# A gated short-convolution layer in fp32 halves: adaLN's scales and features moved directly behind their totals, the opening passes' products reordered, the first low part moved ahead, and the load of conv_w held back

## The chip, the cores and the metric

The kernel runs on one NeuronCore of one Trainium2 chip. The metric is the device time of one execution in microseconds (us), as the median of several runs. Before the change it is 913.54 us, the median of three runs (913.52 to 914.13).

## What is computed

The layer has one batch row, 256 positions, 2048 channels (`D`) and a branch width of 4096 (`E`). Cut to what matters, in NumPy-like words:

```python
h = rmsnorm(x, norm_g)                                   # (256, 2048)
shift, scale, gate = split(silu(c) @ ada_w + ada_b, 3)   # ada_w: (2048, 3*2048)
h = h * (1 + scale) + shift
b_gate, c_gate, v, g = split(h @ w_in, 4)                # w_in: (2048, 4*4096)
u = causal_conv3(c_gate * v, conv_w)                     # per channel, 3 taps
y = b_gate * u * silu(g)
out = rmsnorm(x + gate * (y @ w_out), final_g)           # w_out: (4096, 2048)
```

All tensors are fp32. `w_in` alone is 128 MB, so the weights are streamed once from HBM.

## The kernel before, in words

**Products in three parts.** Every weight tile that lands from HBM (`raw`, 128 rows by 2048 columns) is split into a high part (`hi`, a copy in the fp32r format on ACT, `high()`, line 603) and a low part (`lo = raw - hi` on DVE, `low()`, line 610). The features h are kept in the same way as a high and a low half of the tile `hT`. One product of a 128x128 weight block with 256 positions is then three matmuls: high weights by high features, high weights by low features, and low weights by high features (`product()`, line 507, the matmul itself is line 511). Every matmul has a weight load of its own.

**Why there are passes.** The features of channel block k (128 channels; there are 16) can only be made when the shift and the scale of that block are known, and these need their columns of `ada_w`, another 32 MB that come in during the first third of the kernel. So the first half of `w_in`'s columns is worked off in passes over the channel blocks whose features are ready: first k = 0 and 1 for every column group, then k = 2 and 3, and so on. `plan()` (line 75) fixes these passes. A pass is cut into pieces, one per weight tile, numbered b = 0, 1, 2, ...; pieces 0 and 1 are half tiles. A full piece has 48 matmuls for 128x1024 weights, in two halves of 24 (j = 0 and 1), each half into a PSUM bank of its own. The passes that begin at k = 0 are called opening passes here: pieces 0 to 9. Piece 9 is the first that uses k = 2 and 3; piece 14 is the first that uses k = 4 and 5.

**The order inside a half.** In the opening passes (`opening_products()`, line 528) a half does 16 matmuls with the high weights and then 8 with the low weights. In all later ones (`chunk_products()`, line 517) the three matmuls of one weight block follow one another: high, high, low, eight times.

**How features become ready.** `ada_w`'s columns for two channel blocks arrive in eight tiles (`at`); for each, `sum_one()` does two multiply-adds on DVE into `gv` (lines 487 and 489). When the eighth is done, `turn_sums()` puts four transposes on PE (`tp_g`, line 496), `total_sums()` sums the transposed rows on ACT (line 503), `all_scales()` makes scale and shift on DVE (lines 647 to 649), and `all_features()` makes the features: ACT writes the high half of `hT` (line 361), DVE the low half (lines 362 and 363). There are seven such groups of two channel blocks after the first, which is made at the start by another path (lines 398 to 443).

**What sets the order.** Each engine runs its instructions in the order of the program. The loop over pieces (line 731) writes this order out: it is pinned by `in_order()` until all features are made (line 782), and from there on a scheduler chooses. For piece b the loop makes the high part of piece b + 2, some sums, then the scales, the low part of piece b + 2, then the features, and then PE's matmuls for piece b; the transposes and totals come in the middle of the matmuls, after the first half. A clock per engine, kept by `spend()` with fixed costs, decides how many sums go between (`sum_some()`). All loads are issued on the SP queue. After piece 44 the loop also loads the taps `conv_w` as 96 rows of 512 bytes (`rows2`, line 784), and transposes them on PE (line 273) into `cw` (line 275); nothing on the way holds that load, so that the scheduler issues it near the start of the kernel.

After the passes the second half of `w_in`'s columns follows with all 16 channel blocks at once (`mm_b`), and then the product with `w_out` (`mm_o`).

Of the kernel before, what the change touches and what calls it, by code (L numbers as in the profile page):

```python
# [13 lines left out]
P = 128  # L14
# [47 lines left out]
SUM_US = 1.5  # L62
# [91 lines left out]
def short_conv_layer(ctx: ExitStack, tc: tile.TileContext, x, c, norm_g, ada_w, ada_b, w_in, conv_w, w_out, final_g, out):  # L154
# [204 lines left out]
    def features(k, sc, sh):  # L359
        hf = xs[k // CT][:, k % CT, :]  # L360
        nc.scalar.activation(hh_[:, k], hf, AF.Identity, bias=sh, scale=sc)
        nc.vector.tensor_scalar(out=hf, in0=hf, scalar1=sc, scalar2=sh, op0=ALU.mult, op1=ALU.add)
        nc.vector.tensor_tensor(out=hl_[:, k], in0=hf, in1=hh_[:, k].bitcast(F32), op=ALU.subtract)  # L363
# [70 lines left out]
    hi0 = wpool.tile([P, SLOT], F32R, tag="hi", name="hi", bufs=3)  # L434
    lo0 = wpool.tile([P, SLOT], F32R, tag="lo", name="lo", bufs=3)
    w = CT * P
    for k in range(NK0):
        nc.vector.tensor_tensor(out=sh_sc[:, k], in0=sums0[k][:, :, 0], in1=b_both[:, :, k], op=ALU.add)
    for k in range(NK0):
        c = slice(k * w, (k + 1) * w)  # L440
        nc.scalar.copy(hi0[:, c], raw0[:, c])
        nc.vector.tensor_tensor(out=lo0[:, c], in0=raw0[:, c], in1=hi0[:, c].bitcast(F32), op=ALU.subtract)
        features(k, sh_sc[:, k, 1:2], sh_sc[:, k, 0:1])

    def taps(ct, u, cv):

# [52 lines left out]
    def ada_total(nk, tp):  # L499

        gs = const.tile([P, 4], F32, tag="gs", name="gs", bufs=2)
        for o in range(2 * nk):
            nc.scalar.activation(tp[:, o, :], tp[:, o, :], AF.Copy, accum_out=gs[:, o : o + 1])
        return gs[:, 0:nk], gs[:, nk : 2 * nk]
# [130 lines left out]
    def total_sums():  # L635

        while totals:
            k0, nk, tp = totals.pop(0)
            whole_sums.append((k0, nk, ada_total(nk, tp)))
            spend("act", TOTAL_US, clock["pe"])  # L640

    def all_scales():

        while whole_sums:
            k0, nk, (sums_shift, sums_scale) = whole_sums.pop(0)
            ks = slice(k0, k0 + nk)
            nc.vector.tensor_tensor(out=scale[:, ks], in0=sums_scale, in1=b_scale1[:, ks], op=ALU.add)
            nc.vector.tensor_tensor(out=scale[:, ks], in0=scale[:, ks], in1=gT[:, ks], op=ALU.mult)
            nc.vector.tensor_tensor(out=shift[:, ks], in0=sums_shift, in1=b_shift[:, ks], op=ALU.add)
            spend("dve", STALL_US)  # L650
            scaled.append((k0, nk))

    def all_features():
# [77 lines left out]
    for b, (n, chs, q, k0, k1, seeds, w, s0, sk, _) in enumerate(flat):  # L731
        us = sk * len(chs) * CT * 3 * PRODUCT_US
        begin, end = clock["pe"], clock["pe"] + us
        last = s0 + sk == k1
        for e in ("dve", "act"):
            clock[e] = max(clock[e], begin)
        early = b + 2 < N and raws.get((b + 2, "at"), begin) > begin - EARLY_US
        for closing in (early, not early):
            if closing:
                if ended_pass is not None:  # L740
                    close_bank(ended_pass, len(passes[ended_pass][1]) - 1)
                    ended_pass = None
            else:
                nxt = b + 2 < N and high(b + 2)
        if nxt:
            sum_some(nxt[2] + STALL_US, HI_US)
            all_scales()
            low(b + 2, *nxt)
        all_features()
        get_ready(s0 + sk)  # L750
        if last and n + 1 in passes:
            open_bank(n + 1, 0)
            if len(chs) == 1 and len(passes[n + 1][1]) == 2:
                open_bank(n + 1, 1)
        adds = last and len(chs) == 2 and k0 > 0 and not seeds[0]
        sum_some(end + AHEAD_US, STALL_US)
        mix_some(end + AHEAD_US)
        hi, lo = parted.pop(b)
        parted[b] = None
        for j in range(len(chs)):  # L760
            bank = banks[n, j]
            if b == 0:
                for k in range(NK0):
                    chunk_products(bank, hi, lo, k * w, k, k0, k1, late=True)
            elif k0 == 0:
                opening_products(bank, hi, lo, w, j * CT * P, s0, sk, k1)
            else:
                for i in range(sk):
                    chunk_products(bank, hi, lo, i * w + j * CT * P, s0 + i, k0, k1, seeds[j])
            if j == 0:  # L770
                clock["pe"] = begin + us / len(chs)
                turn_sums(clock["pe"] - TURN_US)
                if last and len(chs) == 2:
                    close_bank(n, 0)
                    if n + 1 in passes:
                        open_bank(n + 1, 1)
                total_sums()
        clock["pe"] = end
        if last:
            ended_pass = n  # L780
        if ready[0] == KT:
            pinned.close()
        if b == CONV_AT:
            nc.sync.dma_start(rows2[:, :], conv_w.rearrange("w (k p) -> (w k) p", p=P))
            turn(rows2, 0, 96, cw)
    close_bank(ended_pass, len(passes[ended_pass][1]) - 1)
    for us, do in mixing:
# [221 lines left out]
```

## Time and profile before

| | |
|---|---|
| median of the runs | 913.54 us |
| profiled execution, device time | 913.98 us |
| profiled execution, span of the trace | 912.2 us |
| PE (matmuls) busy | 898.8 us, 99% |
| PE weight loads busy | 860.4 us, 94% |
| DVE busy | 632.9 us, 69% |
| ACT busy | 452.9 us, 50% |
| loaded from HBM | 224.48 MB |

The span is what the trace covers; the device time of the same execution is 1.8 us longer. A time with a dot and two decimals, such as 71.42, is a moment in us from the start of the span. A timeline row gives its start, its length, engine, line, operation, output and inputs and the number of instructions merged into it; in square brackets stands how long the engine sat idle before it and what ended that. PE is busy almost without a break, so the time is to be found in two places: in the few short waits of PE, and in the pace at which matmuls follow one another, which the busy share does not show because successive matmuls overlap.

### The profile page before, as it was taken

The page shows a single profiled execution, that of the slowest core. Times are in us where ns is not written, and L with a number is a line of the kernel's source. Part 1 is how long each engine was busy: PE and PEld are TensorE (multiplying, and loading weights), DVE is VectorE, ACT ScalarE, POOL GpSimd, SP SyncE. Part 2 cuts the span into 40 slices and gives each one's busy share as a digit, 9 for nine tenths or more (in the row PEclk, how much of TensorE's full clock was granted, in tenths as well). Part 3 has the DMA queues.
Part 4 walks back from the last instruction along what each step waited for, and adds up shares of the span by engine and source line. Part 5 has one row for each costly group of instructions (what it writes and reads, how often), then busy time and mean ns, then how long its engine had stood idle before and what let it go on. Part 6 is the DMA issues. An engine that isn't in the chain of part 4 may idle for free.

```text
span 912.2 us, 16163 instructions
## 1 busy us (share of the span) xinstructions
PE 898.8 (99%) x7045; PEld 860.4 (94%) x7045; DVE 632.9 (69%) x603; ACT 452.9 (50%) x430; POOL 1.8 (0%) x8
## 2 busy tenths in 40 slices
PE   7999999999999999999999999999999999999996
PEld 5999999999999999999999999999999988888885
DVE  5788899999646878776666666666566644555882
ACT  6688776545545755643344443334433433433333
POOL 0000000000000000000000000000000000000000
PEclk9999999999999999999999999999999999999999
DMA  9999999999555555797677778777877496565542
GB/s 307 382 381 357 314 364 338 321 345 312 190 197 202 190 190 184 256 299 247 216 255 239 240 219 270 248 238 227 255 239 245 145 356 203 199 204 191 185 139 92
DMA packets 146855, 227.63 MB, mean 250 GB/s; under 512 B 5456, under 2 KB 103904, under 8 KB 146400
## 3 DMA queue, kind: packets, MB, share of 16 engines
q1 hardware_dynamic: 146688, 226.56, 74.4%
q8 instruction: 55, 0.90, 0.4%
q14 instruction: 16, 0.13, 0.0%
q0 software_dynamic: 64, 0.02, 0.0%
q10 hardware_dynamic: 32, 0.01, 0.0%
HBM read 224.48 MB, written 2.10 MB: 248 GB/s over the span
## 4 chain that ended last, share of the span: by engine, by line
PE 91%; DMA 5%; DVE 2%; ACT 1%; issue 0%; ACTq 0%; SPq 0%
PE mm_b L511 38%; PE mm_s L511 33%; PE mm_o L907 6%; PE mm_o L906 6%; PE mm_o L905 6%; DMA at<-in_ada_w_dram 3%; DMA raw_s<-in_sc_w_in_dram 1%; DVE gv L489 1%; DVE lo L610 1%; DMA x<-in_x_dram 1%; ACT hi L603 0%; PE tp_g L496 0%; PE ps_gate L843 0%; DVE acc L545 0%; ACT big L919 0%
## 5 line engine op out<-in xcount | busy, mean ns | idle before, releaser
L511 PE MATMUL mm_b<-hT,hi 128*128 128x256 f32 x2048 | 348.4, 276 | 0.0
L511 PE MATMUL mm_s<-hT,hi 128*128 128x256 f32 x2048 | 338.4, 277 | 1.1 <-DVE hT L363 1.0
L511 PEld LDWEIGHTS mm_b<-hT,hi 128*128 128x128 f32 x2048 | 308.7, 188 | 0.1
L511 PEld LDWEIGHTS mm_s<-hT,hi 128*128 128x128 f32 x2048 | 300.4, 188 | 2.0 <-DVE hT L363 1.7
L511 PE MATMUL mm_b<-hT,lo 128*128 128x256 f32 x1024 | 282.6, 276 | 0.0
L511 PE MATMUL mm_s<-hT,lo 128*128 128x256 f32 x1024 | 263.2, 277 | 0.3 <-DVE lo L610 0.2
L370 DVE TENSOR_TENSOR lo<-raw,hi 128x2048 fp32r<-128x2048 f32 x64 | 146.7, 2292 | 114.9 <-ACT hi L369 114.9
L369 ACT CAST hi<-raw 128x2048 fp32r<-128x2048 f32 x64 | 122.4, 1913 | 197.7 <-PE mm_b L511 142.5
L511 PEld LDWEIGHTS mm_b<-hT,lo 128*128 128x128 f32 x1024 | 192.2, 188 | 0.0
L511 PEld LDWEIGHTS mm_s<-hT,lo 128*128 128x128 f32 x1024 | 183.4, 188 | 0.7 <-DVE lo L610 0.4
L610 DVE TENSOR_TENSOR lo<-raw_s,hi 128x2048 fp32r<-128x2048 f32 (+1 forms) x64 | 145.5, 2273 | 54.0 <-ACT hi L603 52.8
L603 ACT CAST hi<-raw_s 128x2048 fp32r<-128x2048 f32 (+1 forms) x64 | 121.5, 1899 | 105.8 <-PE mm_s L511 85.4
L370 DVE TENSOR_TENSOR lo<-raw_o,hi 128x2048 fp32r<-128x2048 f32 x32 | 73.3, 2290 | 63.6 <-ACT hi L369 63.6
L369 ACT CAST hi<-raw_o 128x2048 fp32r<-128x2048 f32 x32 | 61.0, 1907 | 106.4 <-PE mm_o L907 84.5
L906 PE MATMUL mm_o<-lo,y 128*128 128x512 f32 x256 | 99.3, 389 | 0.0
L907 PE MATMUL mm_o<-hi,y 128*128 128x512 f32 x256 | 99.3, 389 | 0.0
L905 PE MATMUL mm_o<-hi,y 128*128 128x512 f32 x256 | 99.3, 389 | 0.0
L489 DVE SCALAR_TENSOR_TENSOR gv<-at,silu_c,gv 128x512 f32<-128x512 f32 x105 | 78.8, 750 | 2.7
L906 PEld LDWEIGHTS mm_o<-lo,y 128*128 128x128 f32 x256 | 48.1, 188 | 10.0
L905 PEld LDWEIGHTS mm_o<-hi,y 128*128 128x128 f32 x256 | 48.1, 188 | 10.0
L907 PEld LDWEIGHTS mm_o<-hi,y 128*128 128x128 f32 x256 | 48.1, 188 | 9.9
L543 ACT COPY acc<-mm_s 128x1024 f32<-128x1024 f32 x43 | 43.2, 1013 | 12.7 <-PE mm_s L511 12.7
(106 smaller groups left out, 377.4 us busy)
## 6 DMA issues: line engine op xcount, KB each, us to landing
raw<-in_sc_w_in_dram SPq DMA_DIRECT2D x64, 1024.0 KB, 6.7
raw_s<-in_sc_w_in_dram SPq DMA_DIRECT2D x63, 1024.0 KB, 6.7
raw_o<-in_sc_w_out_dram SPq DMA_DIRECT2D x32, 1024.0 KB, 5.2
at<-in_ada_w_dram SPq DMA_DIRECT2D x126, 256.0 KB, 7.2
at_g<-in_ada_w_dram SPq DMA_DIRECT2D x32, 512.0 KB, 7.6
x<-in_x_dram SPq DMA_DIRECT2D x4, 512.0 KB, 6.5
big<-in_x_dram SPq DMA_DIRECT2D x2, 1024.0 KB, 7.5
out_dram<-big SPq DMA_DIRECT2D x4, 512.0 KB, 2.9
```

The lines of the kernel that those rows point to most:

```text
L369: nc.scalar.copy(hi[:, :n], raw[:, :n])
L370: last_low[0] = nc.vector.tensor_tensor(out=lo[:, :n], in0=raw[:, :n], in1=hi[:, :n].bitcast(F32), op=ALU.subtract)
L489: nc.vector.scalar_tensor_tensor(out=gv, in0=at4[:, i], scalar=c_k, in1=gv, op0=ALU.mult, op1=ALU.add)
L511: mm = last_mm[0] = nc.tensor.matmul(dst, w, h[:, k], start=begins and left, stop=ends, skip_group_check=True)
L543: nc.scalar.copy(acc[ch, q], bank)
L603: nc.scalar.copy(hi[:, :n], raws[b][:, :n])
L610: nc.vector.tensor_tensor(out=lo[:, :n], in0=raws.pop(b)[:, :n], in1=hi[:, :n].bitcast(F32), op=ALU.subtract)
L905: nc.tensor.matmul(po, yh, hi[:, o], start=opens, stop=False, skip_group_check=True)
L906: nc.tensor.matmul(po, yh, lo[:, o], start=False, stop=False, skip_group_check=True)
L907: nc.tensor.matmul(po, yl, hi[:, o], start=False, stop=ct == NCT - 1, skip_group_check=True)
```

## The change

Five things are done.

1. `all_scales()` and `all_features()` are called directly behind `total_sums()`, in the middle of piece b's matmuls, and no longer in the next turn of the loop around the low part of piece b + 2. `all_scales()` now knows when its totals are ready and first does such sums as fit in before (`at`).
2. With that, the rest of the sums (`sum_some(end + AHEAD_US, ...)`) and of the mixing (`mix_some`) move behind these calls, and a smaller part (`sum_some(begin + us / len(chs), ...)`) stays ahead of the matmuls.
3. `opening_products()` is only used for b + j < 4, that is for piece 1, both halves of piece 2 and the first half of piece 3. All later halves of the opening passes use `chunk_products()`.
4. For the first two channel blocks at the start, DVE makes the low weights of block 0 before the second sum, and not behind it.
5. The load of `conv_w`'s rows is ordered behind the last weight load issued so far.

```diff
-    for k in range(NK0):
+
+    def first_sums(k):
         nc.vector.tensor_tensor(out=sh_sc[:, k], in0=sums0[k][:, :, 0], in1=b_both[:, :, k], op=ALU.add)
-    for k in range(NK0):
+
+    def first_parts(k):
         c = slice(k * w, (k + 1) * w)
         nc.scalar.copy(hi0[:, c], raw0[:, c])
         nc.vector.tensor_tensor(out=lo0[:, c], in0=raw0[:, c], in1=hi0[:, c].bitcast(F32), op=ALU.subtract)
-        features(k, sh_sc[:, k, 1:2], sh_sc[:, k, 0:1])
+
+    first_sums(0)
+    first_parts(0)
+    first_sums(1)
+    features(0, sh_sc[:, 0, 1:2], sh_sc[:, 0, 0:1])
+    first_parts(1)
+    features(1, sh_sc[:, 1, 1:2], sh_sc[:, 1, 0:1])
...
-            whole_sums.append((k0, nk, ada_total(nk, tp)))
-            spend("act", TOTAL_US, clock["pe"])
+            whole_sums.append((k0, nk, ada_total(nk, tp), spend("act", TOTAL_US, clock["pe"])))
...
-            k0, nk, (sums_shift, sums_scale) = whole_sums.pop(0)
+            k0, nk, (sums_shift, sums_scale), at = whole_sums.pop(0)
+            while waiting and max(clock["dve"], waiting[0][2]) + SUM_US <= at + STALL_US:
+                sum_one()
...
-            spend("dve", STALL_US)
+            spend("dve", STALL_US, at)
...
             sum_some(nxt[2] + STALL_US, HI_US)
-            all_scales()
             low(b + 2, *nxt)
-        all_features()
         get_ready(s0 + sk)
...
-        sum_some(end + AHEAD_US, STALL_US)
-        mix_some(end + AHEAD_US)
+        sum_some(begin + us / len(chs), STALL_US)
...
-            elif k0 == 0:
+            elif k0 == 0 and b + j < 4:
                 opening_products(bank, hi, lo, w, j * CT * P, s0, sk, k1)
...
                 total_sums()
+                all_scales()
+                all_features()
+                sum_some(end + AHEAD_US, STALL_US)
+                mix_some(end + AHEAD_US)
...
-            nc.sync.dma_start(rows2[:, :], conv_w.rearrange("w (k p) -> (w k) p", p=P))
+            load = nc.sync.dma_start(rows2[:, :], conv_w.rearrange("w (k p) -> (w k) p", p=P))
+            tc.add_manual_dep(load.ins, last_load[0].ins.name, after, reason="behind this piece's load")
             turn(rows2, 0, 96, cw)
```

The number of matmuls, weight loads, vector and scalar operations and loads is the same before and after. What moves is shown at three places. The numbers behind names tell tiles of one name apart.

First PE, in pieces 3 and 4 (`hi_335` and `lo_343` are the weights of piece 3, `hi_375` and `lo_382` those of piece 4; `mm_s` are the banks). Before:

```order
L511 MATMUL mm_s_386<-hT_164,hi_335 128x256 x16
L511 MATMUL mm_s_386<-hT_164,lo_343 128x256 x8
L511 MATMUL mm_s_413<-hT_164,hi_335 128x256 x16
L511 MATMUL mm_s_413<-hT_164,lo_343 128x256 x8
L511 MATMUL mm_s_456<-hT_164,hi_375 128x256 x16
L511 MATMUL mm_s_456<-hT_164,lo_382 128x256 x8
```

The same place now, with repeated rows left out; the second half of piece 3 and all of piece 4 follow the pattern high, high, low:

```order
L519 MATMUL mm_s_386<-hT_164,hi_335 128x256 x16
L519 MATMUL mm_s_386<-hT_164,lo_343 128x256 x8
L519 MATMUL mm_s_413<-hT_164,hi_335 128x256 x2
L519 MATMUL mm_s_413<-hT_164,lo_343 128x256
...
L519 MATMUL mm_s_456<-hT_164,hi_375 128x256 x2
L519 MATMUL mm_s_456<-hT_164,lo_382 128x256
```

From the second half of piece 3 to the end of piece 9, thirteen halves change their order; a low weight block is now needed by the third matmul of a half and not by the seventeenth.

Second DVE, where the features of k = 4 and 5 are made (`gv_1073` and `gv_1100` are the sums of the group after, `lo_1156` and `lo_1133` the low part of piece 15, `lo_1067` that of piece 14). Before:

```order
L610 TENSOR_TENSOR lo_1067<-raw_s_863,hi_1064 128x2048
L487 TENSOR_SCALAR gv_1073<-at_930,silu_c_132 128x512
L489 SCALAR_TENSOR_TENSOR gv_1073<-at_930,silu_c_132,gv_1073 128x512
L489 SCALAR_TENSOR_TENSOR gv_1073<-at_941,silu_c_132,gv_1073 128x512 x2
L489 SCALAR_TENSOR_TENSOR gv_1073<-at_999,silu_c_132,gv_1073 128x512 x2
L647 TENSOR_TENSOR scale_170<-gs_1116,vec_130 128x2
L648 TENSOR_TENSOR scale_170<-scale_170,vec_130 128x2
L649 TENSOR_TENSOR shift_169<-gs_1116,vec_130 128x2
L610 TENSOR_TENSOR lo_1156<-raw_s_935,hi_1145 128x2048
L362 TENSOR_SCALAR xs1_166<-xs1_166,scale_170,shift_169 128x256
L363 TENSOR_TENSOR hT_164<-xs1_166,hT_164 128x256
```

The same place now:

```order
L618 TENSOR_TENSOR lo_1062<-raw_s_858,hi_1059 128x2048
L497 SCALAR_TENSOR_TENSOR gv_712<-at_897,silu_c_132,gv_712 128x512 x2
L495 TENSOR_SCALAR gv_1100<-at_962,silu_c_132 128x512
L497 SCALAR_TENSOR_TENSOR gv_1100<-at_962,silu_c_132,gv_1100 128x512
L618 TENSOR_TENSOR lo_1133<-raw_s_930,hi_1130 128x2048
L656 TENSOR_TENSOR scale_170<-gs_1166,vec_130 128x2
L657 TENSOR_TENSOR scale_170<-scale_170,vec_130 128x2
L658 TENSOR_TENSOR shift_169<-gs_1166,vec_130 128x2
L362 TENSOR_SCALAR xs1_166<-xs1_166,scale_170,shift_169 128x256
L363 TENSOR_TENSOR hT_164<-xs1_166,hT_164 128x256
```

The low part of piece 15 has gone from between the scales and the features to ahead of the scales, and the last two sums of this group (`gv_712`) now stand behind the low part of piece 14. With that, PE's four transposes for this group move back by one piece: they stood in the middle of piece 12, and stand in the middle of piece 13 now, 24 matmuls ahead of the first that needs k = 4. Those of the first group (k = 2 and 3) stay in the middle of piece 7.

Third the SP queue, at the load of `conv_w`'s rows. Before, it stood near the start:

```order
L583 DMA raw_s_277<-in_sc_w_in_dram 128x2x512
L583 DMA raw_s_279<-in_sc_w_in_dram 128x2x1024
L474 DMA at_281<-in_ada_w_dram 128x2x256 x2
L583 DMA raw_s_284<-in_sc_w_in_dram 128x2x1024
L474 DMA at_286<-in_ada_w_dram 128x2x256 x2
L784 DMA rows2_83<-in_sc_conv_w_dram 96x128
L583 DMA raw_s_293<-in_sc_w_in_dram 128x2x1024
```

Now it stands directly behind the load of piece 49 (`raw_s_3163`):

```order
L591 DMA raw_s_2996<-in_sc_w_in_dram 128x2x1024
L591 DMA raw_s_3055<-in_sc_w_in_dram 128x2x1024
L591 DMA raw_s_3109<-in_sc_w_in_dram 128x2x1024
L591 DMA raw_s_3163<-in_sc_w_in_dram 128x2x1024
L794 DMA rows2_83<-in_sc_conv_w_dram 96x128
L591 DMA raw_s_3221<-in_sc_w_in_dram 128x2x1024
```

It has passed 46 weight loads and all later `at` loads on that queue. The transpose of these rows on PE, which stood between pieces 44 and 45, now stands behind the first matmul of piece 46.

## The prediction

> **What bounds the kernel now.** The page comes first: its span, and the busy shares.
>
> ```profile
> span 912.2 us, 16163 instructions
> PE 898.8 (99%) x7045; PEld 860.4 (94%) x7045; DVE 632.9 (69%) x603; ACT 452.9 (50%) x430; POOL 1.8 (0%) x8
> ```
>
> PE has no idle time to speak of, so what can be won is its few waits and its pace. The waits of PE between 30 and 381 us (the stage the change touches) are these three, 1.2 us in all:
>
> ```profile
> PE mm_s L511 <- DVE hT L363: 1.0, 2, 0.8
> PE mm_s L511 <- DVE lo L610: 0.2, 1, 0.2
> ```
>
> The pace shows in the busy time by stretches (length, then PE busy with its instructions):
>
> ```profile
> 40.00:50.00 10.00, 10.00 (x86) 10.00 (x86) 9.02 (x9) 7.58 (x7) 0.00 (x0) 1.00 1.05 381
> 272.00:381.00 109.00, 109.00 (x964) 109.00 (x963) 79.76 (x83) 65.72 (x64) 0.00 (x0) 1.00 0.62 203
> ```
>
> Both stretches are full at a granted clock of 1.00, yet the first runs 8.6 matmuls per us and the second 964 / 109 = 8.84. The timeline of PE shows where pace and waits change (start, length):
>
> ```profile
> 30.71 2.09 PE L511 MATMUL mm_s<-hT,hi 128*128 128x256 f32 x16
> ...
> 39.78 2.16 PE L511 MATMUL mm_s<-hT,hi 128*128 128x256 f32 x16
> ...
> 42.72 2.04 PE L511 MATMUL mm_s<-hT,hi 128*128 128x256 f32 x16
> ...
> 45.54 2.04 PE L511 MATMUL mm_s<-hT,hi 128*128 128x256 f32 x16
> ...
> 62.86 2.13 PE L511 MATMUL mm_s<-hT,hi 128*128 128x256 f32 x16
> ...
> 65.77 2.04 PE L511 MATMUL mm_s<-hT,hi 128*128 128x256 f32 x16
> ...
> 68.60 2.04 PE L511 MATMUL mm_s<-hT,hi 128*128 128x256 f32 x16
> ...
> 71.42 0.28 PE L511 MATMUL mm_s<-hT,hi 128*128 128x256 f32 x1
> 71.96 1.99 PE L511 MATMUL mm_s<-hT,hi 128*128 128x256 f32 x15 [0.26 <-DVE hT L363]
> ...
> 74.70 1.98 PE L511 MATMUL mm_s<-hT,hi 128*128 128x256 f32 x16
> ...
> 77.42 0.39 PE L511 MATMUL mm_s<-hT,hi 128*128 128x256 f32 x2
> ...
> 91.02 0.60 PE L496 MATMUL tp_g<-ident,gv 128*128 128x128 f32 x4
> 91.38 0.48 PE L511 MATMUL mm_s<-hT,hi 128*128 128x256 f32 x2
> ...
> 92.53 0.39 PE L511 MATMUL mm_s<-hT,hi 128*128 128x256 f32 x2
> ...
> 92.87 0.39 PE L511 MATMUL mm_s<-hT,hi 128*128 128x256 f32 x2
> ...
> 99.67 0.28 PE L511 MATMUL mm_s<-hT,hi 128*128 128x256 f32 x1
> 100.70 0.39 PE L511 MATMUL mm_s<-hT,hi 128*128 128x256 f32 x1 [0.75 <-DVE hT L363]
> ...
> 101.04 0.40 PE L511 MATMUL mm_s<-hT,hi 128*128 128x256 f32 x2
> ```
>
> A half of 24 matmuls takes 45.54 - 42.72 = 2.82 us in piece 4, and 77.42 - 74.70 = 2.72 us in piece 9, in the same old order. So there are two paces, 118 and 113 ns per matmul. The slow one holds until the wait at 71.42, and the fast one from there.
>
> **The features moved forward, pieces 9 and 14.** Piece 9's first half takes 74.70 - 71.42 = 3.28 us, 0.56 over 2.72. Piece 14 loses more: three matmuls from 99.67 to 101.04 take 1.37 where 3 x 0.113 = 0.34 is due, a loss of 1.03. On DVE the reason stands in the rows, a low part in front of the features:
>
> ```profile
> 68.83 2.29 DVE L610 TENSOR_TENSOR lo<-raw_s,hi 128x2048 fp32r<-128x2048 f32 x1 [0.44 <-ACT hi L603]
> 71.48 0.43 DVE L363 TENSOR_TENSOR hT<-xs,hT 128x256 fp32r<-128x256 f32 x1
> ...
> 97.24 0.15 DVE L647 TENSOR_TENSOR scale<-gs,vec 128x2 f32<-128x2 f32 x1
> ...
> 97.51 0.16 DVE L649 TENSOR_TENSOR shift<-gs,vec 128x2 f32<-128x2 f32 x1
> 97.58 2.29 DVE L610 TENSOR_TENSOR lo<-raw_s,hi 128x2048 fp32r<-128x2048 f32 x1
> 99.78 0.41 DVE L362 TENSOR_SCALAR xs<-xs,scale,shift 128x256 f32<-128x256 f32 x1
> 100.22 0.42 DVE L363 TENSOR_TENSOR hT<-xs,hT 128x256 fp32r<-128x256 f32 x1
> ```
>
> For piece 9 the change takes that low part (2.29 us) and the four sums ahead of it out of the way, while the transposes stay in the middle of piece 7, before 62.86. The features come some 4 us ahead of PE and the wait goes: **0.56 us gained**. Next late there would be piece 9's low part, on DVE before 68.83 in either order.
>
> For piece 14 the transposes move 48 matmuls back, so the chain must be added up. It is taken from the group whose totals began at once:
>
> ```profile
> 147.48 0.60 PE L496 MATMUL tp_g<-ident,gv 128*128 128x128 f32 x4
> ...
> 148.11 0.26 ACT L503 ACTIVATE tp_g<-tp_g 128x128 f32<-128x128 f32 x1 [1.35 <-PE tp_g L496]
> ...
> 149.49 0.20 ACT L503 ACTIVATION_READ_ACCUMULATOR tp_g<-tp_g 128x1 f32 x1
> ```
>
> With the transposes starting at t, the totals end at t + (149.69 - 147.48) = t + 2.21. Scales and shift take 97.67 - 97.24 = 0.43 more, and DVE's two steps for k = 4 take 100.64 - 99.78 = 0.86. With about 0.1 for handing over, the low half of hT is there at t + 3.6. PE passes the transposes in 91.38 - 91.02 = 0.36 and needs 2.85 for the 24 matmuls left (91.38 to 92.87 for twelve, 1.36 for twelve more). Its first matmul for k = 4 is due at t + 3.21, and the second, which reads the low half, at t + 3.33. So PE still waits 0.3 us, or 0.4 with a slow restart, where it lost 1.03: **0.6 us gained**. DVE must be free at t + 2.2. The low part of piece 15 ahead of the scales can begin when piece 12 is done and its high part made (t - 2.7 + 1.9), and so ends at t + 1.5. The bounds are a gain of 1.0 if the chain is quicker, and a loss of 0.8 if that low part comes a whole 2.29 late (1.8 waited over 0.7 of margin, beside 1.03).
>
> **High, high, low in pieces 3 to 9.** From 39.78 to 71.42 eleven halves run at the slow pace. If the new order runs them at the fast one, that is 11 x (2.82 - 2.72) = **1.1 us gained**. Does the order set the pace? In the old order a break does not always end the slow pace: behind the transposes at 62.86 the halves still take 65.77 to 68.60, 2.83. In the later passes, which have the new order, each break is followed by some nine slower matmuls (91.38 to 92.53, 1.15 us) and then by three in 0.34 (92.53 to 92.87). The bounds are 0 and 1.1; if only the break at 62.86 helps, it is 3 x 0.1 = 0.3. I take 1.1, because no half in the new order keeps the slow pace in this trace, although none starts from it without a break either.
>
> The Trainium skill (TensorE: Matmul & The Clock Gate, section "Wait — 56ns, not 53.3ns?") speaks against that term: it puts a warm stream at N / 2.4 GHz plus about 2.5 ns per matmul, a fixed cost behind the decoder, so about 109 ns for 256 columns whatever the order. By it the sum would lack the 1.1 us; the trace agrees with neither side fully, since it shows 118 and 113 ns and no 109.
>
> A low block needed at a half's third matmul costs nothing: DVE's low parts lie a full piece ahead of PE. That is piece 9's case above, needed at 71.42 and made before 68.83.
>
> **The start.** The first low part made sooner speeds up pieces 0 and 1 only. PE's next work, piece 2, waits for a load, ACT's high part and nothing else:
>
> ```profile
> 28.75 1.91 ACT L603 CAST hi<-raw_s 128x2048 fp32r<-128x2048 f32 x1 [2.62 <-DMA raw_s<-in_sc_w_in_dram]
> ```
>
> It ends at 30.66, and PE began piece 2 at 30.71. So the gain is 0, between 0 and 0.1; PE idles sooner instead.
>
> **The rows of conv_w.** They now follow the load of piece 49, and PE's transpose of them stands at the start of piece 46. In the old run that load is issued here; then come the time of such loads to landing in that stretch (255 to 300 us), and that of the rows at the start:
>
> ```profile
> 270.80 0.37 SPq L583 DMA_DIRECT2D raw_s<-in_sc_w_in_dram  x1
> raw_s<-in_sc_w_in_dram SPq DMA_DIRECT2D x7, 1024.0 KB, 5.2
> rows<-in_sc_conv_w_dram SPq DMA_DIRECT2D x1, 48.0 KB, 10.3
> 271.85 0.25 PE L273 MATMUL tp_v<-ident,rows 96*128 96x96 f32 x1
> ```
>
> The transpose stood ahead of piece 45, at 271.85; two halves later (5.44) and 0.1 on is 277.4. The rows land between 271.2 + 5.2 = 276.4 and 271.2 + 10.3 = 281.5, so PE waits between 0 and 4.1 us. I take 0: the queue is slack there, and the 10.3 belongs to a full one. Without that cover every us of lateness is a us of the end.
>
> **The sum.** 0.56 + 0.6 + 1.1 = 2.26 us, and later stages keep it, since PE is full from 102 us on. The profiled execution took 913.98 (span 912.2), which gives 911.7; it lies 0.44 above the median of the runs, from which the forecast is 913.54 - 2.26 = **911.3 us**. A measurement of this kernel can tell 0.2%, 1.8 us, from no change: faster ends at 911.7, slower begins at 915.4.
>
> **The rivals.**
> - *Pace without the order* (chance 0.25). The slow pace is a state of the early stretch that ends by a wait, as at 71.42; with that wait gone it may even last longer. For it: the same order ran at both paces. Only 0.56 + 0.6 remain, and 0.3 at most: 912.1 to 912.4.
> - *The second group too late* (0.1). Its transposes stand 24 matmuls before their use. If DVE is late by a low part, the loss of 0.8 replaces the 0.6: 913.54 - 0.56 - 1.1 + 0.8 = 912.7. Against it: 0.7 us of margin.
> - *Slower, by conv_w's rows* (0.08). If they take 10.3 us to land, PE stands 4.1 us at piece 46: 911.3 + 4.1 = 915.4. It turns the whole change at 2.26 us of waiting, a landing 8.5 us after the issue. Against it: 5.2 for loads twenty times as big.
> - *Nothing moves* (0.05): 913.5, if other waits take the place of these.
>
> **How the numbers follow.** The forecast has 0.52 (its own range 910.9 to 911.9). With 911.7 as the bound, most of it counts as faster and the rest, with the first two rivals, as no change: faster 0.5, same 0.43, slower 0.07. The range takes in the forecast with the whole of piece 14's wait gone (910.7), the first rival, and the second (912.8).
>
> **What would show it.** PE would show no wait near 70 us, one of 0.2 to 0.4 near 98, halves of 2.72 us from 40 us on, and nothing before the transpose near 275. It is wrong if halves still take 2.82 at 50 us, or if PE waits in pieces 10 to 46 for anything else.

## The result and the profile after

The changed kernel takes 912.48 us against 914.0 us for the kernel before (medians of 22 runs each, taken in turn). The ratio is 0.9983 (95% interval 0.9976 to 0.9989), a gain of 1.5 us (1.0 to 2.2). That is clear of zero, and at 0.17% just below the 0.2% that the prediction named as its bound; the interval reaches past it. The profiled execution took 911.95 us, 2.03 less than that of before.

The page of the changed kernel, span and busy time:

```profile
span 910.2 us, 16162 instructions
PE 897.1 (99%) x7045; PEld 859.1 (94%) x7045; DVE 633.5 (70%) x603; ACT 453.1 (50%) x430; POOL 1.8 (0%) x8
```

Its waits of PE between 30 and 381 us (total, times, longest):

```profile
PE mm_s L519 <- DVE hT L363: 0.5, 1, 0.5
PE mm_s L519 <- DVE lo L618: 0.2, 1, 0.2
PE mm_s L519 <- ACT acc L551: 0.2, 1, 0.2
```

One of the two waits for features is gone, the other is still there, and one for a bank is new. The busy time by stretches:

```profile
40.00:50.00 10.00, 10.00 (x89) 9.93 (x88) 8.98 (x9) 7.54 (x7) 0.00 (x0) 1.00 1.05 383
272.00:381.00 109.00, 109.00 (x964) 109.00 (x963) 81.53 (x86) 65.90 (x64) 0.00 (x0) 1.00 0.62 203
```

Between 40 and 50 us PE does 89 matmuls where it did 86; the late stretch has 964 as before. PE's timeline at the places of the prediction:

```profile
29.97 0.73 PE L519 MATMUL mm_s<-hT,hi 128*128 128x256 f32 x5
...
39.22 0.39 PE L519 MATMUL mm_s<-hT,hi 128*128 128x256 f32 x1 [0.19 <-ACT acc L551]
...
69.91 0.28 PE L519 MATMUL mm_s<-hT,hi 128*128 128x256 f32 x1
...
72.63 0.39 PE L519 MATMUL mm_s<-hT,hi 128*128 128x256 f32 x2
...
75.35 0.39 PE L519 MATMUL mm_s<-hT,hi 128*128 128x256 f32 x2
...
94.40 0.60 PE L504 MATMUL tp_g<-ident,gv 128*128 128x128 f32 x4
...
97.75 0.38 PE L519 MATMUL mm_s<-hT,hi 128*128 128x256 f32 x1
98.66 0.38 PE L519 MATMUL mm_s<-hT,hi 128*128 128x256 f32 x1 [0.53 <-DVE hT L363]
...
101.41 0.39 PE L519 MATMUL mm_s<-hT,hi 128*128 128x256 f32 x2
```

The two traces side by side, as starts in us, show where the 2.05 came from:

| start of | before | after | gained in between |
|---|---|---|---|
| piece 2 | 30.71 | 29.97 | 0.74 |
| second half of piece 3 | 39.78 | 39.22 | -0.18 |
| piece 9 | 71.42 | 69.91 | 0.95 (the pace) |
| second half of piece 9 | 74.70 | 72.63 | 0.56 (its wait) |
| piece 15 | 106.18 | 104.13 | -0.02 (piece 14: nothing) |

From there on the two run alike; at piece 37 the gap is 2.04 us (227.83 and 225.79).

Why piece 14 gained nothing stands on ACT and DVE. First ACT's row for these features in the kernel before, then ACT and DVE in the changed kernel, and the weight load of piece 14's first matmul:

```profile
97.94 1.10 ACT L361 ACTIVATE hT<-xs,shift,scale 128x256 fp32r<-128x256 f32 x2
```

```profile
95.03 0.26 ACT L511 ACTIVATE tp_g<-tp_g 128x128 f32<-128x128 f32 x1 [0.45 <-PE tp_g L504]
...
96.40 0.19 ACT L511 ACTIVATION_READ_ACCUMULATOR tp_g<-tp_g 128x1 f32 x1
97.09 1.09 ACT L361 ACTIVATE hT<-xs,shift,scale 128x256 fp32r<-128x256 f32 x2 [0.50 <-DVE shift L658]
```

```profile
93.71 2.29 DVE L618 TENSOR_TENSOR lo<-raw_s,hi 128x2048 fp32r<-128x2048 f32 x1
96.63 0.16 DVE L656 TENSOR_TENSOR scale<-gs,vec 128x2 f32<-128x2 f32 x1 [0.63 <-ACT tp_g L511]
...
96.90 0.15 DVE L658 TENSOR_TENSOR shift<-gs,vec 128x2 f32<-128x2 f32 x1
97.73 0.41 DVE L362 TENSOR_SCALAR xs<-xs,scale,shift 128x256 f32<-128x256 f32 x1 [0.67 <-ACT hT L361]
98.18 0.43 DVE L363 TENSOR_TENSOR hT<-xs,hT 128x256 fp32r<-128x256 f32 x1
```

```profile
97.75 0.19 PEld L519 LDWEIGHTS mm_s<-hT,hi 128*128 128x128 f32 x1 [0.17 <-ACT hT L361]
```

DVE is free from 96.0 on and waits for ACT, first 0.63 us for the totals and then 0.67 us for ACT's high half of hT. From the transposes to the matmul that needs the low half it takes 98.66 - 94.40 = 4.26 us. PE had work for only 3.21: piece 14's first matmul began 0.25 us behind the one before it, where 0.11 is the pace, because its weight load waited for ACT's high half. So PE waited twice on this chain, some 0.14 us for the high half and 0.53 for the low one. The first of the two is counted in the half behind the transposes, which takes 3.00 us and not the 2.86 of the kernel before.

The rows of conv_w in the changed kernel, their issue on SP, their time to landing in the last column, and PE's transpose:

```profile
269.18 0.46 SPq L794 DMA_DIRECT2D rows<-in_sc_conv_w_dram  x1
```

```profile
rows<-in_sc_conv_w_dram SPq DMA_DIRECT2D x1, 48.0 KB, 5.1
```

```profile
275.36 0.25 PE L273 MATMUL tp_v<-ident,rows 96*128 96x96 f32 x1
```

They land at 269.18 + 5.1 = 274.3, 1.1 us ahead of their use, and PE waits for nothing there.

### The profile page after: what moved, and what is told of

It is laid out like the page before. It is cut to its first block, busy times and chain, and to the rows that moved or that the text cites. A ratio compares the mean times of both kernels' runs of the same rounds, so it can differ in the third digit from the quotient of the medians.

```text
span 910.2 us, 16162 instructions
## 1 busy us (share of the span) xinstructions
PE 897.1 (99%) x7045; PEld 859.1 (94%) x7045; DVE 633.5 (70%) x603; ACT 453.1 (50%) x430; POOL 1.8 (0%) x8
## 4 chain that ended last, share of the span: by engine, by line
PE 95%; DMA 3%; ACT 1%; DVE 1%; SPq 0%; issue 0%; ACTq 0%
PE mm_b L519 38%; PE mm_s L519 37%; PE mm_o L917 6%; PE mm_o L918 6%; PE mm_o L916 6%; DMA at<-in_ada_w_dram 2%; DMA raw_s<-in_sc_w_in_dram 1%; DMA raw<-in_sc_w_in_dram 0%; PE tp_g L504 0%; ACT hi L611 0%; PE ps_gate L854 0%; SPq L236 0%; ACT tp_g L511 0%; DVE lo L444 0%; DVE lo L618 0%
## 5 line engine op out<-in xcount | busy, mean ns | idle before, releaser
L519 PE MATMUL mm_s<-hT,hi 128*128 128x256 f32 x2048 | 347.2, 277 | 0.7 <-DVE hT L363 0.5
L519 PEld LDWEIGHTS mm_s<-hT,hi 128*128 128x128 f32 x2048 | 306.5, 188 | 1.5 <-DVE hT L363 0.7
L519 PE MATMUL mm_s<-hT,lo 128*128 128x256 f32 x1024 | 277.5, 276 | 0.2 <-DVE lo L618 0.2
L519 PEld LDWEIGHTS mm_s<-hT,lo 128*128 128x128 f32 x1024 | 189.8, 188 | 0.4 <-DVE lo L618 0.4
```

What stands on the lines that cost most here:

```text
L519: mm = last_mm[0] = nc.tensor.matmul(dst, w, h[:, k], start=begins and left, stop=ends, skip_group_check=True)
```

## The experiments

Theory: three things act separately, the pace in pieces 3 to 8 (set by the order), the wait at piece 9, and a chain at piece 14 that is longer than the work left to PE; what happens ahead of piece 4 is chance. Rivals stand with each run. One table first. Times are medians; the ratio is to runs of the kernel before on the same chip, taken in turn; the last three columns are from one trace of each kernel: start of PE's first product, start of the second half of piece 3, and the stretch from the start of piece 4 to that of piece 15.

| kernel | us | ratio (95%) | first | piece 3, 2nd half | pieces 4 to 14 |
|---|---|---|---|---|---|
| before | | | 24.25 | 39.78 | 63.46 |
| changed | 912.48 | 0.9983 (0.9976 to 0.9989) | 24.30 | 39.22 | 62.07 |
| order_alone | 913.47 | 0.9993 (0.9985 to 1.0002) | 24.22 | 39.47 | 62.76 |
| old_order_rest_new | 913.28 | 0.9991 (0.9982 to 1.0000) | 25.81 | 39.71 | 63.14 |
| features_alone | 913.89 | 0.9998 (0.9990 to 1.0007) | 24.21 | 39.63 | 63.16 |
| rows_held_alone | 913.87 | 1.0001 (0.9992 to 1.0010) | 25.07 | 39.50 | 63.54 |
| late_two_runs | 912.48 | 0.9981 (0.9972 to 0.9990) | 24.38 | 39.39 | 62.04 |
| four_high_two_low | 912.64 | 0.9984 (0.9975 to 0.9993) | 24.52 | 39.35 | 62.66 |
| second_group_sooner | 911.18 | 0.9966 (0.9954 to 0.9979) | 25.92 | 39.75 | 60.88 |
| rows_early_rest_new | 912.99 | 0.9987 (0.9978 to 0.9995) | 24.37 | 39.99 | 62.17 |
| two_runs_from_15 | 912.28 | 0.9983 (0.9974 to 0.9992) | 24.06 | 39.46 | 62.10 |
| first_part_old_rest_new | 912.59 | 0.9985 (0.9977 to 0.9994) | 25.69 | 40.12 | 61.93 |
| sooner_piece3_new_order | 911.53 | 0.9976 (0.9966 to 0.9986) | 24.00 | 39.36 | 60.98 |
| changed_again | 912.57 | 0.9983 (0.9974 to 0.9992) | 25.71 | 39.94 | 62.07 |

**The order alone**, in the kernel before:

```diff
-            elif k0 == 0:
+            elif k0 == 0 and b + j < 4:
```

> The kernel before with one edit: from the second half of piece 3 on, the opening passes have the order high, high, low. Theory 'the order ends the slow pace': the halves of pieces 4 to 8 take 2.72 us and not 2.83, so piece 9 begins about 1.0 us sooner (near 70.4), the wait for its features grows by as much as it comes sooner unless DVE is earlier too, so that 0.5 to 1.0 of the gain is lost there, and the time is 0 to 0.6 us under the kernel before. Rival 'a wait ends the slow pace': in the changed kernel the fast pace began at a wait at 39.22 us, which this kernel need not have; its halves then stay at 2.83 until the wait at piece 9, and the time is that of the kernel before within 0.2 us.

Busy time by stretches, 47 to 58 us, and PE at piece 9:

```profile
47.00:58.00 11.00, 11.00 (x100) 11.00 (x99) 9.92 (x11) 8.98 (x8) 0.00 (x0) 1.00 1.05 382
```

```profile
70.13 0.28 PE L511 MATMUL mm_s<-hT,hi 128*128 128x256 f32 x1
70.89 0.39 PE L511 MATMUL mm_s<-hT,hi 128*128 128x256 f32 x1 [0.48 <-DVE hT L363]
```

From 39.47 to 70.13 it takes 30.66 us where the kernel before took 31.64: 0.98 gained by the order alone. Piece 9's first half then takes 3.51 and not 3.28, so 0.23 of it is waited away again. This is the first theory's case, in the trace; the time alone, 913.47 us, is not clear of the kernel before (the interval of its ratio reaches 1.0002). A wait for a bank stands at 39.47 here too, which leaves room for the rival; but at 45.09 one matmul took 143 ns to the next with no wait in the trace, nine more came every 115 to 122 ns, and from then on they were back at 113. The new order leaves the slow pace without a wait.

**The order put back**, in the changed kernel:

```diff
-            elif k0 == 0 and b + j < 4:
+            elif k0 == 0:
```

> The changed kernel with the order of the opening passes put back (16 matmuls with high weights, then 8 with low ones). Theory 'the order ends the slow pace': the halves from 39 us to the end of piece 9 take 2.83 us, 13 x 0.11 = 1.4 us more than in the changed kernel, since no wait at piece 9 breaks the pace now. Rival 'a wait ends the slow pace': if the wait for a bank at 39.22 us stands here too, the halves behind it take 2.72 and the time is that of the changed kernel within 0.2 us.

The same stretch, and PE at pieces 9 and 10:

```profile
47.00:58.00 11.00, 11.00 (x96) 11.00 (x95) 10.05 (x11) 9.01 (x8) 0.00 (x0) 1.00 1.05 382
```

```profile
71.35 0.52 PE L519 MATMUL mm_s<-hT,hi 128*128 128x256 f32 x3
...
74.18 0.40 PE L519 MATMUL mm_s<-hT,hi 128*128 128x256 f32 x2
...
77.00 0.40 PE L519 MATMUL mm_s<-hT,hi 128*128 128x256 f32 x2
...
79.74 0.39 PE L519 MATMUL mm_s<-hT,hi 128*128 128x256 f32 x2
```

96 matmuls against 100, both stretches full at a granted clock of 1.00. The halves take 2.83 (74.18 - 71.35) up to the end of piece 9. From piece 4 to 15 it takes 1.07 us more than the changed kernel, a little less than the 1.4 expected, and the time is 913.28, 0.8 over it. The wait for a bank did not occur here, since PE came later. What refutes the rival stands at piece 10, the first that has the order high, high, low in this kernel too: its first three matmuls came every 117 to 120 ns, those from the fourth on every 113 to 114, and the half took 79.74 - 77.00 = 2.74 us. PE waited for nothing there. The traces of features_alone and rows_held_alone show the same at their piece 10. The gap at 45.09 in order_alone, beside the same gap in rows_held_alone below, points the same way.

**Scales and features alone**, in the kernel before (with the sums moved as in the change):

```diff
-            all_scales()
             low(b + 2, *nxt)
-        all_features()
...
                 total_sums()
+                all_scales()
+                all_features()
```

> The kernel before with one edit: scales and features directly behind their totals, and the sums moved with them. Theory 'piece 9 gains, piece 14 does not': the wait of 0.56 us at piece 9 goes, but with it the break that ended the slow pace, so that its two halves take 2.83 each (0.22 lost); piece 14's first half takes 3.6 to 3.7 as in the changed kernel, since its transposes stand 24 matmuls ahead and the chain behind them is 4.3 us long; the time is 0.3 us under the kernel before (0.1 to 0.6). Rival 'piece 14 gains 0.6 as forecast, and it was lost again elsewhere in the changed kernel': piece 14's first half takes 3.1 to 3.2, and the time is 0.9 to 1.2 us under the kernel before.

PE at piece 9 and at piece 14:

```profile
71.27 0.40 PE L511 MATMUL mm_s<-hT,hi 128*128 128x256 f32 x2
...
74.10 0.52 PE L511 MATMUL mm_s<-hT,hi 128*128 128x256 f32 x3
...
76.92 0.40 PE L511 MATMUL mm_s<-hT,hi 128*128 128x256 f32 x2
...
99.34 0.38 PE L511 MATMUL mm_s<-hT,hi 128*128 128x256 f32 x1
100.25 0.38 PE L511 MATMUL mm_s<-hT,hi 128*128 128x256 f32 x1 [0.53 <-DVE hT L363]
```

The wait at piece 9 is gone, and both halves take 2.83, so that the piece takes 5.65 (76.92 - 71.27) where it took 6.00. Piece 14 waits the same 0.53 as in the changed kernel. From piece 4 to piece 15 this part gains 0.30 and the order 0.70; together they gain 1.39. Each takes away what the other lost: the order's wait at piece 9, and the slow pace in piece 9, which in the trace of the kernel before had ended at the old wait. These are figures of one trace each; by its time, 913.89 us, this kernel can't be told from the kernel before.

**conv_w's rows held, alone**, in the kernel before:

```diff
-            nc.sync.dma_start(rows2[:, :], conv_w.rearrange("w (k p) -> (w k) p", p=P))
+            load = nc.sync.dma_start(rows2[:, :], conv_w.rearrange("w (k p) -> (w k) p", p=P))
+            tc.add_manual_dep(load.ins, last_load[0].ins.name, after, reason="behind this piece's load")
```

> The kernel before with one edit: the load of conv_w's rows is ordered behind the load of piece 49. Theory 'the rows crowd the opening': the load of piece 2 lands near 27.9 us and not 28.75, PE begins piece 2 near 29.9 and not 30.71, a wait for a bank in piece 3 gives some 0.3 us back, and the time is 0.4 to 0.6 us under the kernel before. Rival 'chance': the earlier landing in the changed kernel's trace was a scatter of the loads; piece 2 begins at 30.7 and the time is that of the kernel before within 0.2 us. In both, PE has no wait at the transpose near 275 us.

Two stretches of this kernel, and PE at the start of piece 4's second half and of the one after it, and at pieces 9 and 10:

```profile
34.00:44.00 10.00, 10.00 (x90) 10.00 (x90) 8.98 (x9) 6.92 (x7) 0.00 (x0) 1.00 1.06 382
47.00:58.00 11.00, 11.00 (x96) 11.00 (x95) 9.63 (x10) 9.03 (x8) 0.00 (x0) 1.00 1.05 382
```

```profile
44.94 0.43 PE L511 MATMUL mm_s<-hT,hi 128*128 128x256 f32 x2
...
47.80 0.52 PE L511 MATMUL mm_s<-hT,hi 128*128 128x256 f32 x3
...
70.85 0.28 PE L511 MATMUL mm_s<-hT,hi 128*128 128x256 f32 x1
71.39 2.04 PE L511 MATMUL mm_s<-hT,hi 128*128 128x256 f32 x15 [0.26 <-DVE hT L363]
...
74.20 2.04 PE L511 MATMUL mm_s<-hT,hi 128*128 128x256 f32 x16
...
77.03 0.40 PE L511 MATMUL mm_s<-hT,hi 128*128 128x256 f32 x2
```

No gain: the rival "chance" holds for the time, though not in its details: piece 2 began at 31.34, since PE's first product came only at 25.07. The trace gave something else: the old order at the fast pace (90 matmuls in 10 us) through pieces 2 and 3 and the first half of piece 4, and at the slow one from 44.94 on. One matmul there followed the other after 149 ns and not 113, and from the next on they came every 118 ns up to the end of piece 9. In order_alone the same gap, at the same matmul, was over after ten. So the old order is not slow by itself, but here it keeps the slow pace once it has it.

The wait at piece 9 did not end the slow pace here, though it was as long as in the kernel before (0.26 us idle in both): the half behind it still took 77.03 - 74.20 = 2.83 us. That the fast pace set in behind this wait in the kernel before is thus what one trace showed, not what such a wait does each time.

**conv_w's rows early**, in the changed kernel (the same edit backwards):

```diff
-            load = nc.sync.dma_start(rows2[:, :], conv_w.rearrange("w (k p) -> (w k) p", p=P))
-            tc.add_manual_dep(load.ins, last_load[0].ins.name, after, reason="behind this piece's load")
+            nc.sync.dma_start(rows2[:, :], conv_w.rearrange("w (k p) -> (w k) p", p=P))
```

> The changed kernel with the load of conv_w's rows free again, near the start. Theory 'the rows cost nothing that lasts': the stretch from piece 4 on is that of the changed kernel (62.1 us from the start of piece 4 to that of piece 15), and the time is that of the changed kernel within 0.3 us. Rival 'they hold up the load of piece 4': the second half of piece 3 begins 0.4 us later or more, counted from the start of piece 2's load, and the time is 0.3 to 0.7 us over the changed kernel.

The stretch is 62.17, 0.1 over the changed kernel; the second half of piece 3 began 0.77 later than there, at 39.99, but the second run of the changed kernel has it at 39.94. The four kernels with early rows have it at 39.47 to 39.99, the ten with late ones at 39.22 to 40.12. Counted from the start of piece 2's load, as the rival has it, the half began after 19.00 us, against 18.30 and 18.67 in the two traces of the changed kernel. The time, 912.99 us, is 0.5 over the 912.48 of the changed kernel, outside the 0.3 of the theory and within the rival's 0.3 to 0.7; but the intervals of the two ratios overlap, and holding the rows alone gained nothing (1.0001). So an effect of the rows can't be told from chance; it is not over some tenths of a us, and the rival is not refuted.

**The old order late in the program**, pieces 41 to 59 of the changed kernel:

```diff
...
-            elif k0 == 0 and b + j < 4:
+            elif k0 == 0 and b + j < 4 or 41 <= b < 60:
...
```

The lines left out tell `opening_products()` where a bank's sum begins.

> The changed kernel with the order of 16 high and 8 low matmuls per half also in pieces 41 to 59, far behind the opening, where the loads are slack; the transpose of conv_w's rows stands in between, in piece 46. Theory 'a break starts the slow pace, and only the order high, high, low ends it': the halves of pieces 41 to 45 take 2.72 us as before, and from the transpose on to the end of piece 59 they take 2.83, so the time is about 27 x 0.11 = 3.0 us over the changed kernel. Rival 'the slow pace belongs to the opening' (its loads, or what DVE and ACT do there): all halves take 2.72 but for the one with the transpose, and the time is that of the changed kernel within 0.3 us. Second rival 'the old order is slow by itself, whatever went before': slow from piece 41 on, 3.9 to 4.2 us over the changed kernel.

Two stretches, ahead of the transpose of conv_w's rows and behind it:

```profile
248.00:268.00 20.00, 20.00 (x178) 20.00 (x178) 10.23 (x5) 9.69 (x6) 0.00 (x0) 1.00 0.63 211
281.00:355.00 74.00, 74.00 (x656) 74.00 (x655) 57.65 (x65) 47.59 (x49) 0.00 (x0) 1.00 0.59 198
```

The changed kernel has 179 and 655 there. The theory that a break starts the slow pace in the old order fell for this break, and the second rival fell with it.

**The old order from piece 15 on**, with five groups of transposes at the start of a half:

```diff
...
-            elif k0 == 0 and b + j < 4:
+            elif k0 == 0 and b + j < 4 or 15 <= b < 60:
...
```

> The changed kernel with 16 high and 8 low matmuls per half in pieces 15 to 59, so that five groups of transposes (behind 840, 1080, 1368, 1608 and 1848 matmuls) break the old order exactly at the start of a half, as they did at 62.5 us in the kernel before, where the slow pace went on; the earlier run from piece 41 on had its only break 18 matmuls into a half. Theory 'a break at the start of a half leaves the slow pace in place': from the first of them on the halves take 2.83 us up to piece 45 or 59, 58 to 84 halves x 0.11 = 6 to 9 us over the changed kernel. Rival 'the slow pace lasts only in the opening': each break costs 0.5 us as in the changed kernel and all other halves take 2.72; the time is that of the changed kernel within 0.4 us.

A stretch with the third of these groups in it, and with the DMA engines as full as in the opening (1.04 in the last column but one; 1.05 between 40 and 50 us):

```profile
165.00:190.00 25.00, 25.00 (x223) 25.00 (x223) 22.61 (x28) 15.88 (x20) 0.00 (x0) 1.00 1.04 362
```

The changed kernel has 223 matmuls there too. Behind the transposes the old order is back at 113 ns within some three matmuls, where the new one needs about ten; all five halves behind them take 2.82 against 2.86. So neither the order, nor such a break, nor full DMA engines make the slow pace alone. But PE ran at 113 ns ahead of all five breaks, whereas it ran at 118 ahead of the transposes at 62.5 us, where the slow pace went on. Whether the old order would keep the slow pace late in the program, once in it, no run shows.

**Another order in the opening**, four high and two low:

```diff
...
+            terms = [(i, m, t) for i in range(sk) for g in range(0, CT, 2) for ts in ((0, 1), (2,)) for m in (g, g + 1) for t in ts]
...
```

> The changed kernel with another order in the opening from the second half of piece 3 on: for two weight blocks four matmuls with high weights, then two with low ones. Theory 'low weights every few matmuls end the slow pace': the halves behind the first break take 2.72 us, and the time is that of the changed kernel within 0.2 us. Rival 'only the exact pattern of three on one block ends it': they stay at 2.83 up to piece 9, as in the kernel with the old order, 1.2 to 1.4 us over the changed kernel.

PE behind its wait in piece 4, and a stretch:

```profile
45.54 0.50 PE L519 MATMUL mm_s<-hT,hi 128*128 128x256 f32 x2 [0.45 <-ACT acc L553]
...
48.43 0.50 PE L519 MATMUL mm_s<-hT,hi 128*128 128x256 f32 x3
...
51.15 0.50 PE L519 MATMUL mm_s<-hT,hi 128*128 128x256 f32 x3
```

```profile
49.00:59.00 10.00, 10.00 (x91) 10.00 (x90) 9.31 (x9) 7.98 (x7) 0.00 (x0) 1.00 1.06 379
```

Behind the wait the half takes 2.89 and the next ones 2.72. Low weights every six matmuls do as well as every three. The 0.6 that pieces 4 to 14 take longer in this trace is this wait, for a bank that ACT was still emptying; the median of the runs is only 0.2 over the changed kernel's.

**The second group sooner**, four sums moved ahead:

```diff
+        for _ in range({8: 1, 9: 1, 10: 2}.get(b, 0)):
+            sum_one()
```

> The changed kernel with four sums for k = 4 and 5 made sooner (one each ahead of pieces 8 and 9, two ahead of piece 10), so that the transposes of this group stand in the middle of piece 12 again, a whole piece sooner. Theory 'the chain from transposes to features is 4.3 us long, and 3.3 us of work stood between': PE has no wait at piece 14, whose first half takes 2.72 us and not 3.67, and the half behind the transposes 2.86 and not 3.00; the time is 1.1 us under the changed kernel. Rival 'DVE is the bound there': the sums push the low parts of pieces 12 to 15 back, and PE waits for one of them (for 0.5 to 2 us), or the features still come late because DVE is busy; the time is that of the changed kernel or over it.

PE from its transposes to piece 14:

```profile
89.27 0.49 PE L504 MATMUL tp_g<-ident,gv 128*128 128x128 f32 x3
...
97.91 0.39 PE L519 MATMUL mm_s<-hT,hi 128*128 128x256 f32 x2
...
100.63 0.39 PE L519 MATMUL mm_s<-hT,hi 128*128 128x256 f32 x2
```

Piece 14's first half takes 2.72, and the trace has no wait of PE between 30 and 381 us at all. From piece 12 to the middle of piece 14 it needs 14.09 us (86.54 to 100.63) where the changed kernel needs 15.18: the 1.09 of the theory. This version beats both kernels: 911.18 us, the median of 5 runs.

**The start put back**, in the changed kernel, all of item 4:

```diff
-    first_sums(0)
-    first_parts(0)
-    first_sums(1)
-    features(0, sh_sc[:, 0, 1:2], sh_sc[:, 0, 0:1])
...
+    for k in range(NK0):
+        nc.vector.tensor_tensor(out=sh_sc[:, k], in0=sums0[k][:, :, 0], in1=b_both[:, :, k], op=ALU.add)
+    for k in range(NK0):
...
```

> The changed kernel with the start put back (the first low part behind the second sum). Theory 'the loads bound the start': piece 0 takes 3.5 us and not 2.95, piece 2 begins not over 0.3 us later, the second half of piece 3 between 39.2 and 39.8 as in the other kernels, and the time is that of the changed kernel within 0.2 us. Rival 'the sooner low part is worth its 0.6 us': the second half of piece 3 begins at 39.8 or later, and the time is 0.4 to 0.6 us over the changed kernel.

Piece 0 takes 3.55 us (2.95 in the changed kernel), and the time is the same, 912.59 against 912.57. Its second half of piece 3 began at 40.12, behind a first product at 25.69; the changed kernel, when it too began late (25.71), has 39.94. So 0.6 us at piece 0 leave at most 0.2 by piece 3. The starts did not fall where the theory had them: piece 2 began 0.6 us later than in that second trace (31.96 and 31.36), not 0.3, and 40.12 lies outside 39.2 to 39.8. What speaks for it is the time.

**Piece 3 in the new order as well**, on top of the second group sooner:

```diff
-            elif k0 == 0 and b + j < 4:
+            elif k0 == 0 and b < 3:
```

> The kernel with the second group sooner, and the first half of piece 3 in the order high, high, low as well. Theory 'the load of piece 4 sets the second half of piece 3': the half takes 2.72 us and not 2.83, and PE waits that much longer for the bank behind it; no gain, the time is that of the kernel with the second group sooner within 0.2 us, 911.0 to 911.5, 1.0 to 1.3 under the changed kernel. Rival 'PE's pace sets it': 0.1 to 0.3 us less than that kernel.

911.53 us, not to be told from 911.18, and 1.0 under the changed kernel beside it. The half took 2.81 us and not the 2.72 expected, and the next began at 39.36: nothing was gained there.

**The changed kernel again.**

> The changed kernel once more, as the measure for the other three on the same chip: 912.2 to 912.8 us. Its halves from piece 4 to piece 8 take 2.72 us apart from single gaps, and the first half of piece 14 takes 3.67, if the first trace was typical; if that trace was a chance, the sum of pieces 4 to 14 (62.07 us there) differs by over 0.3.

Its pieces 4 to 14 take 62.07 us, as in the first trace. The start is what differs: its first product began 1.4 us later, and 0.7 of that was left at the second half of piece 3.

## Why the prediction was right, and where it was wrong

The direction and the wide range held, 912.48 us; the forecast's own range, 910.9 to 911.9, did not. The gain is 1.5 us and not 2.26, and one term accounts for most of the difference. The rest of the distance to 911.3 is that the kernel before itself took 914.0 in these runs and not 913.54.

By the time alone this can't be told from the first rival, which said 912.1 to 912.4 and would have lost the order's term. The traces tell them apart: the order's term was had, and piece 14's was lost. That the time came out near the rival's is chance.

- **Piece 9: right.** 0.56 forecast, 0.56 measured; the features were there at 67.16, 2.75 us ahead of PE and not some 4. Alone this part gained 0.35 there, because in the trace of the kernel before the fast pace had set in behind the wait, and without the wait the slow pace went on; the rival "pace without the order" had named that ("may even last longer"). The new order covers it.
- **The order: right in size, half right in reason.** 1.1 forecast, 0.95 in the trace and 0.98 alone. "No half in the new order keeps the slow pace" held in every run, but for some ten matmuls behind a break. But the order does not set the pace by itself: the old one ran at 113 ns in pieces 2 and 3 of rows_held_alone and in pieces 15 to 59. The old order keeps the slow pace, if it has it, until a break ends it, and not every break does; orders with early low weights leave it by themselves. The rival's "ends by a wait, as at 71.42" held in the kernel before and not in rows_held_alone, and its claim that the pace would not change fell with order_alone. That the slow pace is a state of the early stretch, as the rival said, is not shown.
- **Piece 14: wrong.** 0.6 forecast, -0.02 measured. The step that failed is "DVE's two steps for k = 4 take 100.64 - 99.78 = 0.86": between the shift and these two stands ACT's high half of hT, which `xs` waits for. In the kernel before it had run (97.94) beside the low part of piece 15 on DVE (97.58 to 99.87), and the forecast read off DVE's steps with their cover. In the changed kernel DVE waits 0.67 us for it; with t the start of the transposes, the low half is there at t + 4.21 (98.18 + 0.43 - 94.40) and not t + 3.6, and the first matmul of the piece is held up by the high half as well, which the forecast had not asked about. The totals (t + 2.2) and PE's due time (t + 3.21) were right, and DVE was not late, as the forecast had it; second_group_sooner shows that the term was to be had with the transposes one piece sooner.
- **The start: right that it counts for nothing that lasts.** The first trace began piece 2 0.74 sooner, but first products between 24.0 and 25.9 end in second halves of piece 3 between 39.2 and 40.1 in all fourteen traces, and the edits don't sort them.
- **conv_w's rows: right.** No wait, a landing after 5.1 us, 1.1 us to spare.

With piece 14 at nothing the sum is 1.5 to 1.7 (0.56 and 0.95 measured, or 0.56 and 1.1 forecast). The stretch from piece 4 to 15 shows 63.46 - 62.07 = 1.39, the same in both traces of the changed kernel; the rest of the profiled 2.03 lies ahead of piece 4, where executions scatter by as much.

## What to carry to other kernels

When a step is moved, write down the chain on all engines, and look for every instruction that ran beside something in the old trace: it comes back as soon as its cover is moved. A wait and a pace that meet at the same place can't be priced one by one; taking both away gained 1.39 where the single edits gained 0.30 and 0.70, in one trace each. On an engine that is full, count instructions per us: its busy share says nothing of a pace that is 4% off.

## What the runs showed of the hardware

A stream of 128x256 matmuls, each with a weight load, has two steady paces at a granted clock of 1.00: 113 and 118 ns from start to start. The difference lies between a weight load and its matmul: at both paces a load begins some 3 ns behind the start of the matmul before it, but its own matmul begins 110 ns behind it at the fast pace and 114 to 117 at the slow one (before, old_order_rest_new and rows_held_alone). Why is open.

The stream can drop to the slow pace after a gap of only 36 ns (rows_held_alone, 44.94 us), and then stay there in the order of 16 high and 8 low: for eleven halves there, through the wait at piece 9, and for thirteen in old_order_rest_new. In that order a wait switched it either way: in the kernel before from 113 to 118 ns at 33.03 us, and back at 71.42. In the opening the orders with low weights every three or six matmuls returned after about ten matmuls behind a break, and at piece 10, with no break, the order high, high, low returned after three. From piece 15 on the old order returned too, within three matmuls behind transposes that it met at the fast pace. What starts the slow pace is open: full DMA engines and the granted clock don't tell the opening from later, and no run had a wait, or the slow pace itself, late in the old order.

The Trainium skill (TensorE: Matmul & The Clock Gate, section "Wait — 56ns, not 53.3ns?") gives a fixed cost of about 2.5 ns on top of N / 2.4 GHz; the estimate from it was 109 ns for 256 columns. The runs differ: no stretch here was better than 113 ns (223 matmuls in 25 us, in either order), and there is a second pace, which that section does not have. It does not speak of the order of the matmuls.
